# Small products on two halves of the PE array taken in turn, and two groups of transfers moved, in a two-layer hybrid block

## Chip, cores and metric

One core of a Trainium2 chip. The metric is the device time of one execution in microseconds; of several runs the median is given.

## What is computed

Two layers of a block with three token mixers in parallel, 256 tokens by 1024 features, in float32. The reference, cut to what matters here:

```python
for l in range(DEPTH):
    p = x @ w_in[l]
    y_a = rwkv7_time_mix(p[..., :o_mla], ...)      # linear attention with a state per head
    y_b = mla_branch(p[..., o_mla:o_s5], ...)      # causal softmax attention on latents
    y_c = s5_branch(p[..., o_s5:o_gate], ...)      # complex diagonal scan
    gates = jax.nn.sigmoid(p[..., o_gate:].reshape(bsz, t, N_BRANCHES, D_MODEL) + gate_b[l])
    merged = gates[..., 0, :] * y_a + gates[..., 1, :] * y_b + gates[..., 2, :] * y_c
    x = layer_norm(DEEPNORM_ALPHA * x + merged @ w_out[l], ln1_g[l], ln1_b[l])
    h = jax.nn.silu(x @ ffn_w1[l]) * (x @ ffn_w3[l])
    x = layer_norm(DEEPNORM_ALPHA * x + h @ ffn_w2[l], ln2_g[l], ln2_b[l])
```

In `rwkv7_time_mix` the decay and the step size come from two low-rank products (`tanh(dw) @ w2`, `da @ a2`), and the recurrence runs over the tokens; the kernel does it in chunks, with scores between the tokens of a chunk. In `s5_branch` the inputs of the scan are `einsum('btgc,gpc->btgp', ug, bb)`, real and imaginary, with 16 channels to a group.

## The kernel before

**Weights.** All weights come as 276 chunks of 128 x 1024 float32 (512 KB; eight of 416 KB), in the order in which they are used. `w_load` (L155 on) issues a chunk's transfer on SP's queue into `raw` (L160, three buffers), ACT casts it into `whi` (L161, four buffers), and DVE subtracts the two into `wlo` (L171; a part on POOL, L173). `w_next` keeps four chunks ahead. Each product with a weight is three PE products in turn, high by high, low by high, high by low (L206 to L208 in `mm3`; L510 to L512 in `token_major`). SP's queue is in order: what stands before a weight transfer holds it up.

**Order.** The program text gives each engine its order after a scheduler of the tile framework has placed the instructions; two tables of short names, ORDER1 (first half of a layer: the input projection and the scan) and ORDER2 (the linear attention, the attention, the outputs), say in which order generators are advanced, one pair for each layer. In ORDER1 `m` is the latents, `S0 S1` the projection of u, `P` and `T0` to `T4` the scan's tables, `N` the norm of the latents, `r0` to `r6` projections of the linear attention, `t0` to `t3` the first part of `s5_tile`, `w0` to `w3` its second part, `g` and `G` gates. `issue_after` keeps the instructions in its block behind a given one.

**Scan.** `s5_in` projects u and copies it on ACT, and when both halves are there shuffles u into `U2` by eight small transfers on SP's queue (L695), so that two groups of channels lie on rows 0 to 63 and two on rows 64 to 127. `s5_tables` makes the scan's tables: for layer 0 in the head of the kernel, with a chain of rotations on POOL (L385 to L389) and spreads of the B and C matrices on ACT (`bd`, `cd`, L418); for layer 1 during ffn1 of layer 0. Their temporary memory is used afterwards by others, `lg`, `lb` and `xk` among them. `s5_tile(F)` makes eight products of 64 rows (L726), four on the upper row half into one PSUM bank of tag `pa`, then four on the lower half into a second one; each bank is multiplied on DVE by the rotation tables (L733 to L736) as soon as its four are there. The tag `pa` has two banks, and all stages share them. A float32 product leaves two records in the trace.

**Linear attention.** For each f of four (two heads of 64 rows each): `prep(f)` makes the two low-rank products, w2 on rows 0 to 63 (L867) and a2 on rows 64 to 127 (L871), each into its own bank, each followed by a Tanh on ACT (L869, L873). `scores(f)` makes four products on the upper half (head 0) into one bank, a copy on ACT into `Mk` (the copies have the line of the helper, L113), masks on POOL (L947), and then the same for the lower half (L940).

**Output and norm.** `token_major` is the product with w_out (8 chunks) and with ffn_w2 (22 chunks) and the layer norm behind it. It loads the norm's gain and offset over 128 partitions (`lg`, L516, `lb`, L517, 512 KB each) and the residual (`xk`, L518, 1 MB: for the first layer's w_out from the input, else from `xd`, the copy that the norm before wrote to DRAM, L537). The text issues them before chunk 2 of w_out and before chunk 12 of ffn_w2; what they depend on is free earlier, and the scheduler places them where it finds room. The core of that (L516 to L518):

```python
            if k == at:
                SY.dma_start(out=lg, in_=lnv[l, ln:ln + 1, :].to_broadcast([128, D]))
                SY.dma_start(out=lb, in_=lnv[l, ln + 1:ln + 2, :].to_broadcast([128, D]))
                SY.dma_start(out=xk, in_=x_dram)
            w = w_next()
```

## Time and profile before

| | us |
|---|---|
| median of 3 runs | 1076.62 |
| the runs | 1078.77, 1067.44, 1076.62 |
| the profiled execution | 1068.97 |
| its span in the trace | 1067.1 |
| PE busy | 1014.2 |
| DVE busy | 784.7 |
| ACT busy | 482.6 |
| POOL busy | 235.2 |

The profile is of one execution: the span runs from the first to the last instruction in the trace, and the time of the execution has 1.9 us around it. "Busy" is the time in which an engine ran at least one instruction; the rest of the span it waited or had nothing to do. PE's matmuls overlap one another, so the time from one start to the next is shorter than the duration of one.

### The profile page before, as it was taken

The page shows a single profiled execution, that of the slowest core. Times are in us where ns is not written, and L with a number is a line of the kernel's source. Part 1 is how long each engine was busy: PE and PEld are TensorE (multiplying, and loading weights), DVE is VectorE, ACT ScalarE, POOL GpSimd, SP SyncE. Part 2 cuts the span into 40 slices and gives each one's busy share as a digit, 9 for nine tenths or more (in the row PEclk, how much of TensorE's full clock was granted, in tenths as well). Part 3 has the DMA queues.
Part 4 walks back from the last instruction along what each step waited for, and adds up shares of the span by engine and source line. Part 5 has one row for each costly group of instructions (what it writes and reads, how often), then busy time and mean ns, then how long its engine had stood idle before and what let it go on. Part 6 is the DMA issues. An engine that isn't in the chain of part 4 may idle for free.

```text
span 1067.1 us, 21219 instructions
## 1 busy us (share of the span) xinstructions
PE 1014.2 (95%) x8560; PEld 912.5 (86%) x8560; DVE 784.7 (74%) x1542; ACT 482.6 (45%) x797; POOL 235.2 (22%) x262
## 2 busy tenths in 40 slices
PE   8799989999999999799999999999999999999997
PEld 7798778888896999798878999778889879999885
DVE  7969978976578778386474998888747876667546
ACT  5544477534244244144325346865334423443431
POOL 2970222300000599500012003221002420000000
PEclk9989999999999999999999999999999999999999
DMA  8442241223385555466536325232234755555562
GB/s 280 156 159 90 91 147 41 92 89 100 93 294 177 197 180 171 162 207 217 185 123 218 126 81 191 79 98 85 76 100 173 252 190 215 183 188 183 179 196 79
DMA packets 47394, 163.86 MB, mean 154 GB/s; under 512 B 5696, under 2 KB 8256, under 8 KB 46400
## 3 DMA queue, kind: packets, MB, share of 16 engines
q1 hardware_dynamic: 47008, 161.98, 45.9%
q8 instruction: 67, 1.10, 0.4%
q10 hardware_dynamic: 288, 0.52, 0.1%
q14 instruction: 31, 0.25, 0.1%
HBM read 156.72 MB, written 4.19 MB: 151 GB/s over the span
## 4 chain that ended last, share of the span: by engine, by line
PE 58%; DVE 17%; POOL 9%; DMA 7%; ACT 5%; issue 3%; SPq 0%; DVEq 0%; ACTq 0%; POOLq 0%
PE mm L208 11%; PE mm L207 10%; PE mm L206 10%; DMA raw<-in_ws 6%; DVE wlo L171 3%; PE mm L511 3%; PE mm L512 3%; PE mm L510 3%; ACT whi L161 3%; DVE z L745 1%; PE pa L726 1%; PE pb L1035 1%; POOL st L387 1%; PE pb L1043 1%; PE pa L940 1%
## 5 line engine op out<-in xcount | busy, mean ns | idle before, releaser
L171 DVE TENSOR_TENSOR wlo<-raw,whi 128x1024 fp32r<-128x1024 f32 (+2 forms) x265 | 333.5, 1262 | 171.8 <-ACT whi L161 169.1
L161 ACT CAST whi<-raw 128x1024 fp32r<-128x1024 f32 (+2 forms) x267 | 277.4, 1043 | 379.8 <-PE mm L207 211.8
L206 PE MATMUL mm<-xh,whi 128*128 128x256 f32 x1312 | 376.9, 287 | 14.2 <-ACT whi L161 13.9
L208 PE MATMUL mm<-xh,wlo 128*128 128x256 f32 x1312 | 376.1, 287 | 2.9 <-DVE wlo L171 2.6
L207 PE MATMUL mm<-xl,whi 128*128 128x256 f32 x1312 | 375.1, 286 | 0.4 <-DVE xl L262 0.4
L206 PEld LDWEIGHTS mm<-xh,whi 128*128 128x128 f32 x1312 | 249.2, 190 | 18.6 <-ACT whi L161 14.5
L208 PEld LDWEIGHTS mm<-xh,wlo 128*128 128x128 f32 x1312 | 250.2, 191 | 7.6 <-DVE wlo L171 4.0
L207 PEld LDWEIGHTS mm<-xl,whi 128*128 128x128 f32 x1312 | 250.2, 191 | 2.7 <-DVE xl L262 0.6
L240 POOL TENSOR_TENSOR rs<-rs,mhalf 128x1 f32<-128x1 f32 x8 | 7.8, 971 | 341.2 <-DVE rs L238 341.2
L206 PE MATMUL mm<-yh,whi 128*128 128x256 f32 x256 | 74.6, 291 | 0.1
L207 PE MATMUL mm<-yl,whi 128*128 128x256 f32 x256 | 74.1, 289 | 0.0
L208 PE MATMUL mm<-yh,wlo 128*128 128x256 f32 x256 | 74.1, 289 | 0.0
L511 PE MATMUL mm<-wlo,hh 128*128 128x512 f32 x132 | 52.0, 394 | 0.0
L510 PE MATMUL mm<-whi,hh 128*128 128x512 f32 x132 | 51.7, 394 | 0.0
L512 PE MATMUL mm<-whi,hl 128*128 128x512 f32 x132 | 51.5, 392 | 0.0
L206 PEld LDWEIGHTS mm<-yh,whi 128*128 128x128 f32 x256 | 48.5, 189 | 2.3 <-ACT qa L113 0.9
L207 PEld LDWEIGHTS mm<-yl,whi 128*128 128x128 f32 x256 | 48.5, 190 | 1.2 <-issue 0.8
L208 PEld LDWEIGHTS mm<-yh,wlo 128*128 128x128 f32 x256 | 48.6, 190 | 1.1 <-issue 0.7
L240 POOL TENSOR_TENSOR rsn<-rsn,mhalf 128x8 f32<-128x8 f32 x4 | 6.5, 1634 | 142.8 <-DVE rsn L238 142.8
L173 POOL TENSOR_TENSOR wlo<-raw,whi 128x384 fp32r<-128x384 f32 (+2 forms) x24 | 27.7, 1162 | 44.6 <-ACT whi L161 42.5
L947 POOL TENSOR_SCALAR_AFFINE_SELECT Mk<-Mk 64x512 f32<-64x512 f32 x32 | 27.0, 844 | 43.6 <-ACT Mk L113 42.3
L510 PEld LDWEIGHTS mm<-whi,hh 128*128 128x128 f32 x132 | 24.8, 188 | 6.2 <-DVE th L1284 0.8
(487 smaller groups left out, 1745.7 us busy)
## 6 DMA issues: line engine op xcount, KB each, us to landing
raw<-in_ws SPq DMA_DIRECT2D x267, 512.0 KB, 3.8
raw<-in_ws SPq DMA_DIRECT2D x8, 416.0 KB, 3.5
xd<-xk SPq DMA_DIRECT2D x3, 1024.0 KB, 4.1
xk<-xd SPq DMA_DIRECT2D x3, 1024.0 KB, 7.4
lg<-in_lnv SPq DMA_DIRECT2D x4, 512.0 KB, 5.0
lb<-in_lnv SPq DMA_DIRECT2D x4, 512.0 KB, 5.7
pc<-in_spC SPq DMA_DIRECT2D x2, 768.0 KB, 5.3
pb<-in_spB SPq DMA_DIRECT2D x2, 512.0 KB, 4.9
```

What stands on the lines that cost most here:

```text
L161: S.copy(out=hi[:, s], in_=raw[:, s])
L171: V.tensor_tensor(out=lo[:, 0:m], in0=raw[:, 0:m], in1=hi[:, 0:m].bitcast(F32), op=ALU.subtract)
L173: G.tensor_tensor(out=lo[:, m:w], in0=raw[:, m:w], in1=hi[:, m:w].bitcast(F32), op=ALU.subtract)
L206: PE.matmul(ps, lhsT=wh, rhs=xh, start=first, stop=False)
L207: PE.matmul(ps, lhsT=wh, rhs=xl, start=False, stop=False)
L208: PE.matmul(ps, lhsT=wl, rhs=xh, start=False, stop=last)
L240: G.tensor_tensor(out=out, in0=in_, in1=mh(out), op=ALU.pow)
L387: E.tensor_tensor(out=s1, in0=c0, in1=ls, op=ALU.mult)
L510: PE.matmul(acc[b][n], lhsT=ah, rhs=w[0][:, s], start=(k == 0), stop=False)
L511: PE.matmul(acc[b][n], lhsT=ah, rhs=w[1][:, s], start=False, stop=False)
L512: PE.matmul(acc[b][n], lhsT=al, rhs=w[0][:, s], start=False, stop=(k == nk - 1))
L947: G.affine_select(out=Mk[r, h], in_=Mk[r, h], pattern=[[0, 4], [1, 2], [1, 64]], compare_op=ALU.is_ge, fill=0.0, base=-1, channel_multipli ...
```

## The change

Five edits.

1. A helper `in_turn` makes a list of products and chains each behind the one before with `issue_after`. `s5_tile`, `prep` and `scores` take both `pa` banks first and then make their products in turn, one on the upper row half, one on the lower. The DVE work, the Tanhs and the copies follow behind.
2. In ORDER1 of layer 1 `r0` stands before `N t0` instead of behind.
3. The eight shuffles of u are issued on ACT's queue instead of SP's.
4. `token_major` issues its loads behind a chunk's `w_next`, and after the last weight transfer that has been issued; `xk` is split in halves.
5. The loads are spread: in w_out over chunks 0 and 1 (first half of xk and lb; lg and second half), in ffn_w2 over chunks 9, 10, 11 and 12 (first half of xk, lg, lb, second half).

```diff
-    "m S0 S1 P N t0 r0 r1 r2 t1 r3 w0 w1 t2 t3 g0 r4 r5 w2 w3 G3 G1 G2 r6 G0 g1",
+    "m S0 S1 P r0 N t0 r1 r2 t1 r3 w0 w1 t2 t3 g0 r4 r5 w2 w3 G3 G1 G2 r6 G0 g1",
...
+            state["dma"] = SY.dma_start(out=raw[:, s], in_=ws[i, :, s])
...
+    def in_turn(mms):
+
+        last = None
+        for ps, lhsT, rhs in mms:
+            with tc.issue_after(inst(last)) if last is not None else ExitStack():
+                last = PE.matmul(ps, lhsT=lhsT, rhs=rhs, start=True, stop=True)
...
+        loads = [(xk[:, 0], x_dram[:, 0]), (lg, lnv[l, ln:ln + 1, :].to_broadcast([128, D])),
+                 (lb, lnv[l, ln + 1:ln + 2, :].to_broadcast([128, D])), (xk[:, 1], x_dram[:, 1])]
...
-            if k == at:
-                SY.dma_start(out=lg, in_=lnv[l, ln:ln + 1, :].to_broadcast([128, D]))
-                SY.dma_start(out=lb, in_=lnv[l, ln + 1:ln + 2, :].to_broadcast([128, D]))
-                SY.dma_start(out=xk, in_=x_dram)
             w = w_next()
+            if k in at:
+
+                with tc.issue_after(inst(state["dma"])):
+                    for o, i in loads[at.index(k)::len(at)]:
+                        SY.dma_start(out=o, in_=i)
...
-                        SY.dma_start(out=U2[r:r + 32, j // 2::2, :], in_=u[32 * j:32 * j + 32, :, i, :])
+                        S.dma_start(out=U2[r:r + 32, j // 2::2, :], in_=u[32 * j:32 * j + 32, :, i, :])
...
+                pss = [mxps("a"), mxps("a")]
+                in_turn([(pss[pp][:, 256 * qq + 128 * ri:256 * qq + 128 * ri + 128],
+                          bl[64 * pp:64 * pp + 64, 2 * F + qq, ri, :], U2[64 * pp:64 * pp + 64, 2 * F + qq, :])
+                         for qq in range(2) for ri in range(2) for pp in range(2)])
...
+                pss = [mxps("a"), mxps("a")]
+                in_turn([(pss[i][:, 0:256], w2a2[64 * i:64 * i + 64, 128 * f:128 * f + 128], ld[64 * i:64 * i + 64])
+                         for i in range(2)])
...
+                pss = [mxps("a"), mxps("a")]
+                in_turn([(pss[h][:, 128 * b:128 * b + 128],
+                          BK[64 * h:64 * h + 64, b // 2, 2 * (b % 2):2 * (b % 2) + 2].rearrange("p a t -> p (a t)"),
+                          AR[64 * h:64 * h + 64, :, b]) for b in range(4) for h in range(2)])
                 for h in range(2):
...
-            token_major(gate0[1], 8, 0, False, q, l, 2)
+            token_major(gate0[1], 8, 0, False, q, l, [0, 1])
...
-                token_major((hh, hl), NF, 2, l == layers - 1, q2, l, 12)
+                token_major((hh, hl), NF, 2, l == layers - 1, q2, l, [9, 10, 11, 12])
```

The lines of the changed kernel are shifted by 7 to 10: L160 and L161 stay, L206 to L208 become L213 to L215, L418 becomes L425, L518 becomes L529, L695 becomes L705, and all products in turn have the helper's line, L209.

SP's queue from the end of the first w_out to ffn_w2 of layer 0, before (`xd` is the copy of x behind a norm, `pb` an input of layer 1's tables, `raw` a weight chunk):

```order
L537 DMA xd_4219<-xk 128x2048
L160 DMA raw<-in_ws 128x1024 x3
L363 DMA pb<-in_spB 128x1024
L160 DMA raw<-in_ws 128x1024 x23
L516 DMA lg<-in_lnv 128x1024
L517 DMA lb<-in_lnv 128x1024
L518 DMA xk<-xd_4219 128x2048
L160 DMA raw<-in_ws 128x1024 x14
L160 DMA raw<-in_ws 128x832 x2
```
The same stretch of the queue now:

```order
L160 DMA raw<-in_ws 128x1024 x6
L547 DMA xd_4220<-xk 128x2048
L160 DMA raw<-in_ws 128x1024 x3
L370 DMA pb<-in_spB 128x1024
L160 DMA raw<-in_ws 128x1024 x37
L160 DMA raw<-in_ws 128x832 x2
L160 DMA raw<-in_ws 128x1024 x10
L529 DMA xk<-xd_4220 128x1024
L160 DMA raw<-in_ws 128x1024
L529 DMA lg<-in_lnv 128x1024
L160 DMA raw<-in_ws 128x1024
L529 DMA lb<-in_lnv 128x1024
```
Before, the three loads stood behind 23 weight transfers, in ffn1; now the first half of xk, lg, lb and the second half stand behind 49, 50, 51 and 52 transfers, in ffn_w2.

PE around the scores of f = 1 in layer 0, before (`kr__236,BK` are the scores, `ka,qa` products of the attention, `mm` products with weights):

```order
L207 MATMUL mm<-yl,whi 128x256
L926 MATMUL pa<-kr,c 128x256
L208 MATMUL mm<-yh,wlo 128x256
L940 MATMUL pa<-kr__236,BK 128x128 x4
L206 MATMUL mm<-yh,whi 128x256
L207 MATMUL mm<-yl,whi 128x256
L940 MATMUL pa<-kr__236,BK 128x128 x4
L1188 MATMUL pa<-ka,qa 128x128 x2
L208 MATMUL mm<-yh,wlo 128x256
L206 MATMUL mm<-yh,whi 128x256
```
The same scores now, in line L209:

```order
L215 MATMUL mm<-yh,wlo 128x256
L213 MATMUL mm<-yh,whi 128x256
L933 MATMUL pa<-kr,c 128x256
L214 MATMUL mm<-yl,whi 128x256
L209 MATMUL pa<-kr__236,BK 128x128
L215 MATMUL mm<-yh,wlo 128x256
L213 MATMUL mm<-yh,whi 128x256
L214 MATMUL mm<-yl,whi 128x256
L209 MATMUL pa<-kr__236,BK 128x128 x7
L215 MATMUL mm<-yh,wlo 128x256
L213 MATMUL mm<-yh,whi 128x256
```
Before there were two blocks of four, each on one row half, with two weight products between; now the first of the eight stands alone, and the other seven are one block behind three weight products.

ACT in the head of layer 0, before (`u` is the copy of the projection, `bd` and `cd` the spreads of the tables, `kr` a mix of the linear attention's inputs):

```order
L113 COPY u<-mm 128x2x128 x2
L161 CAST whi<-raw 128x1024
L418 ACTIVATE bd<-pb,c 128x32x16
L418 ACTIVATE cd<-pb,c 128x32x16 x2
L161 CAST whi<-raw 128x1024
L418 ACTIVATE bd<-pb,c 128x32x16
L593 ACTIVATE kr__236<-mm,dv 128x256
L418 ACTIVATE bd<-pb,c 128x32x16
L593 ACTIVATE kr__236<-mm,dv 128x256
L418 ACTIVATE cd<-pb,c 128x32x16 x2
L593 ACTIVATE kr__236<-mm,dv 128x256
L161 CAST whi<-raw 128x1024
```
The same part now, with the eight shuffles in it:

```order
L113 COPY u<-mm 128x2x128 x2
L705 DMA U_248<-u 32x4x128 x8
L161 CAST whi<-raw 128x1024 x2
L603 ACTIVATE kr__236<-mm,dv 128x256
L425 ACTIVATE bd<-pb,c 128x32x16
L425 ACTIVATE cd<-pb,c 128x32x16 x2
L603 ACTIVATE kr__236<-mm,dv 128x256
L161 CAST whi<-raw 128x1024
L603 ACTIVATE kr__236<-mm,dv 128x256
L161 CAST whi<-raw 128x1024
L425 ACTIVATE bd<-pb,c 128x32x16
L603 ACTIVATE kr__236<-mm,dv 128x256
```
Two weight casts now stand right behind the eight issues, before the second bd; before, one stood between the u copies and the second bd, the next behind the first pair of cd, and the next only behind the second pair.

## Rows read from the trace of the kernel before

**Rows 1.** The page: busy time, share of the span, instructions.
```profile
PE 1014.2 (95%) x8560; PEld 912.5 (86%) x8560; DVE 784.7 (74%) x1542; ACT 482.6 (45%) x797; POOL 235.2 (22%) x262
```

**Rows 2.** PE's timeline (start, us, line, operation, [idle before <-releaser]), three places.
```profile
51.35 0.58 PE L206 MATMUL mm<-xh,whi 128*128 128x256 f32 x1 [5.62 <-ACT whi L161]
...
453.54 0.58 PE L206 MATMUL mm<-xh,whi 128*128 128x256 f32 x1 [6.83 <-ACT whi L161]
...
581.61 0.68 PE L726 MATMUL pa<-U,bl 64*128 64x128 f32 x4 [2.26 <-DMA U<-u]
```

**Rows 3.** SP's DMA queue, timeline, ffn1 of layer 0.
```profile
426.88 0.33 SPq L160 DMA_DIRECT2D raw<-in_ws  x1
442.81 0.33 SPq L516 DMA_DIRECT2D lg<-in_lnv  x1
...
444.18 10.91 SPq L160 DMA_DIRECT2D raw<-in_ws  x4
```

**Rows 4.** POOL's timeline, the last instruction of the tables.
```profile
441.49 1.29 POOL L389 TENSOR_TENSOR st<-st,t 128x512 f32<-128x512 f32 x1
```

**Rows 5.** Stretch, busy time per engine, PEclk, DMA share, GB/s.
```profile
453.60:458.00 4.40, 3.93 (x17) 3.64 (x18) 4.30 (x7) 2.49 (x4) 0.00 (x0) 0.50 0.36 136
```

**Rows 6.** ACT's timeline, the head and layer 1 after the u copy.
```profile
48.67 1.33 ACT L418 ACTIVATE cd<-pb,c 128x512 f32<-128x512 f32 x2 [4.98 <-DVE pb L408]
...
50.27 1.03 ACT L161 CAST whi<-raw 128x1024 fp32r<-128x1024 f32 x1
...
579.49 1.09 ACT L161 CAST whi<-raw 128x1024 fp32r<-128x1024 f32 x1
```

**Rows 7.** Stretches as in Rows 5, the two scan stages.
```profile
100.00:125.00 25.00, 23.04 (x328) 19.85 (x330) 25.00 (x59) 10.28 (x19) 0.99 (x1) 1.00 0.13 43
...
600.00:650.00 50.00, 48.88 (x593) 44.21 (x592) 48.67 (x101) 20.01 (x31) 5.38 (x5) 1.00 0.32 105
```

**Rows 8.** SP's queue, the U shuffles of both layers.
```profile
33.37 6.92 SPq L695 DMA_DIRECT2D U<-u  x8
...
578.02 5.11 SPq L695 DMA_DIRECT2D U<-u  x8
```

**Rows 9.** POOL's timeline, the end of the rotation.
```profile
69.71 1.28 POOL L389 TENSOR_TENSOR st<-st,t 128x512 f32<-128x512 f32 x1
```

**Rows 10.** PE's timeline, blocks of small products (x counts records).
```profile
76.28 1.71 PE L726 MATMUL pa<-U,bl 64*128 64x128 f32 x16
...
157.96 2.01 PE L940 MATMUL pa<-kr__236,BK 64*128 64x128 f32 x16
...
174.33 1.16 PE L940 MATMUL pa<-kr__236,BK 64*128 64x128 f32 x8
...
583.60 0.71 PE L726 MATMUL pa<-U,bl 64*128 64x128 f32 x4
```

**Rows 11.** PE's timeline, low-rank products beside others.
```profile
122.19 0.48 PE L867 MATMUL pa<-ld,pc 64*128 64x256 f32 x1
122.20 0.48 PE L871 MATMUL pa<-ld,pc 64*128 64x256 f32 x1
...
192.44 0.82 PE L940 MATMUL pa<-kr__236,BK 64*128 64x128 f32 x5
193.00 0.48 PE L867 MATMUL pa<-ld,pc 64*128 64x256 f32 x1
```

**Rows 12.** DVE's timeline, first scan tile of layer 1.
```profile
586.25 0.69 DVE L733 TENSOR_TENSOR pa__6593<-pa,ct 128x512 f32<-128x512 f32 x1 [4.42 <-PE pa L726]
```

**Rows 13.** SP's queue, lg before the first wout.
```profile
292.60 0.33 SPq L160 DMA_DIRECT2D raw<-in_ws  x1
293.71 0.33 SPq L516 DMA_DIRECT2D lg<-in_lnv  x1
```

**Rows 14.** The page: DMA issues, KB each, us to landing.
```profile
xk<-xd SPq DMA_DIRECT2D x3, 1024.0 KB, 7.4
```

**Rows 15.** Instructions of tile Mk: copies out of PSUM, ns min/median/max.
```profile
L113 ACT COPY Mk<-pa x16: 561/586/589, 159.2 to 730.7; 128x512 f32<-128x512 f32 x16
```

More of the change, by code (lines that the diff above doesn't have):

```diff
@@ L159, in w_load @@
         for s in (slice(0, w // 2), slice(w // 2, w)) if i == 0 else (slice(0, w),):
-            SY.dma_start(out=raw[:, s], in_=ws[i, :, s])
+            state["dma"] = SY.dma_start(out=raw[:, s], in_=ws[i, :, s])
             S.copy(out=hi[:, s], in_=raw[:, s])
@@ L721, in s5_tile @@
                 sh4 = [128, 2, 2, 128]
+                pss = [mxps("a"), mxps("a")]
+                in_turn([(pss[pp][:, 256 * qq + 128 * ri:256 * qq + 128 * ri + 128],
+                          bl[64 * pp:64 * pp + 64, 2 * F + qq, ri, :], U2[64 * pp:64 * pp + 64, 2 * F + qq, :])
+                         for qq in range(2) for ri in range(2) for pp in range(2)])
                 for pp in range(2):
-                    ps = mxps("a")
-                    for qq in range(2):
-                        for ri in range(2):
-                            PE.matmul(ps[:, 256 * qq + 128 * ri:256 * qq + 128 * ri + 128],
-                                      lhsT=bl[64 * pp:64 * pp + 64, 2 * F + qq, ri, :],
-                                      rhs=U2[64 * pp:64 * pp + 64, 2 * F + qq, :], start=True, stop=True)
-                    ps4 = ps.rearrange("p (q r t) -> p q r t", q=2, r=2)
+                    ps4 = pss[pp].rearrange("p (q r t) -> p q r t", q=2, r=2)
                     a = q.tile(sh4, F32, tag="pa", name="pa_", bufs=3)
@@ L865, in prep @@
                     pr["bon"] = t1("bon", (128, 2, T), 2)
[L866 to L867 removed]
+                pss = [mxps("a"), mxps("a")]
+                in_turn([(pss[i][:, 0:256], w2a2[64 * i:64 * i + 64, 128 * f:128 * f + 128], ld[64 * i:64 * i + 64])
+                         for i in range(2)])
                 uu = t1("uu")
[L869 to L871 removed]
+                S.activation(out=uu, in_=pss[0][:, 0:256], func=AF.Tanh, bias=hw0[:, f:f + 1], scale=0.5)
                 ta = t1("ta")
[L873 removed]
+                S.activation(out=ta, in_=pss[1][:, 0:256], func=AF.Tanh, bias=ha0[:, f:f + 1], scale=0.5)
                 Gc = t1("Gc", (128, 4, 65))
@@ L935, in scores @@
                 Mk = t1("Mk", (128, 2, 4, 2, 64), NMK)
+                pss = [mxps("a"), mxps("a")]
+                in_turn([(pss[h][:, 128 * b:128 * b + 128],
+                          BK[64 * h:64 * h + 64, b // 2, 2 * (b % 2):2 * (b % 2) + 2].rearrange("p a t -> p (a t)"),
+                          AR[64 * h:64 * h + 64, :, b]) for b in range(4) for h in range(2)])
                 for h in range(2):
-                    o = slice(64 * h, 64 * h + 64)
-                    ps = mxps("a")
-                    for b in range(4):
-                        PE.matmul(ps[:, 128 * b:128 * b + 128],
-                                  lhsT=BK[o, b // 2, 2 * (b % 2):2 * (b % 2) + 2].rearrange("p a t -> p (a t)"),
-                                  rhs=AR[o, :, b], start=True, stop=True)
-                    cp(9, out=Mk[:, h].rearrange("p b a t -> p (b a t)"), in_=ps)
+                    cp(9, out=Mk[:, h].rearrange("p b a t -> p (b a t)"), in_=pss[h])
                     for i in range(2):
```

6 lines of the change are left out of this document (removed).

## Prediction

> **What bounds the kernel now.** I read the busy totals first: TensorE (PE) works 1014.2 of 1067.1 us [rows 1]. So there are only two ways down: fewer microseconds of PE work, or fewer of the some 50 us in which it stands or runs at half clock. Next I looked for the largest idle times in PE's timeline. The largest is 6.83 us, ended at 453.54 by the weight cast on ACT [rows 2]. Followed back through the queues: SP issues a weight transfer at 426.88, and its next instruction, the load of lg, only at 442.81 [rows 3]. In between SP held nothing but a wait, 15.60 us long (442.81 − 426.88 − 0.33). What ended it stands on POOL: the last instruction of the scan tables ends at 441.49 + 1.29 = 442.78 [rows 4], 0.03 us before; lg, lb and xk lie in memory that these tables used. The weight transfers behind lg in SP's queue start at 444.18, and PE ran out of weights. The stall costs more than its length: the granted clock is 0.50 (1.2 GHz) still from 453.6 to 458.0, where PE is again 3.93 of 4.40 us busy [rows 5].
>
> The second largest is 5.62 us at 51.35, in the head, also released by a weight cast [rows 2]. On ACT that cast stands at 50.27 behind two spreads (cd, 1.33 us) that waited 4.98 us for DVE [rows 6]. The third, 2.26 us at 581.61, waits for the shuffled U of layer 1 [rows 2].
>
> Third view, the busy time by stretch: in the two scan stages DVE is full, 25.00 of 25.00 and 48.67 of 50.00 us [rows 7]. PE work saved there is not time saved unless DVE starts sooner.
>
> **Part 1, the late residual loads in ffn2.** In layer 0 lg, lb and xk move from behind 23 weight transfers to behind 49 (one of the four halves after each of four chunks). At 442.78 the tables are done, long before; so the wait of 15.60 us goes, and with it 6.83 us of idle PE. The half clock: from 453.54 to 458.0 PE worked 4.46 us, at 0.50 that is some 2.2 us lost. I take their sum, −9 (bounds −9.5 with the short wait for the first wlo behind it, and −7, the idle time alone). Nothing new is late there: POOL's tables themselves are off the path.
>
> **Part 2, the U transfers from SP to ACT.** Eight issues took 6.92 us of SP's queue in the head and 5.11 us in layer 1 [rows 8], about 0.6 us each with one stall of 2.3 us. On SP the weight transfers stood behind them; on ACT the weight casts, mix-ins and spreads do. In the head the order changes with it: two casts now come before the bd and cd spreads, and the cast that came at 50.27 no longer waits behind cd. What limits the gain is POOL: its rotation chain, which works without a break, ends at 69.71 + 1.28 = 70.99 [rows 9], and the scan can't start before. I take −3.5: the idle 5.62 us and some 1.5 us of half clock, less half for ACT's 5 us of issues, which now delay the casts. Bounds −6 (all of it, and no loss) and +3 (casts 5 us late, two chunks ready). In layer 1, ACT issues eight times right after the u copy; the cast at 579.49 [rows 6] then comes at about 583, some 3.5 us later, where PE takes a new chunk each 3.9 us on the average (276 chunks in 1067 us). Against that r0 is now ahead of N and t0, so PE has some 17 more weight products (a chunk has 24: by the average at most 2.7 us) between u and the scan inputs and hardly meets the 2.26 us. I take 0 (bounds −3 and +4).
>
> A note on the page: the Trainium skill, "DMA: Bandwidth & Descriptors", section "Issuing engines are not separate DMA queues", says that issuing from several engines saves only the sequencer's time to initiate, usually small beside the transfer itself. [Rows 8] show that time to be not small here, 0.6 us an issue, and in a queue with others behind it. By the rule alone this part would be worth nothing, and the sum 3.5 us higher.
>
> **Part 3, the scores in turn.** A block is priced by its rows [rows 10]: 4 records (two products) last 0.71 us, 8 records (four products) 1.16, 16 records, one half and then the other, 2.01 for scores and 1.71 for scan inputs. So one product adds some 0.22 and the first costs some 0.27 more. That the halves run together is seen at 122.19 and 122.20: a product on rows 0 to 63 and one on rows 64 to 127 start 0.01 us apart, and at 193.00 a low-rank product starts inside a score block [rows 11]. Two products in turn then cost as one. Before, by the order of the instructions: two f in one block of eight, five and a half in blocks of four and one pair of twos, 2 × 2.01 + 11 × 1.16 + 2 × 0.71 = 18.2 us. After: seven times 1 + 7 and once 1 + 3 + 4, so eight singles at 0.49, seven at 1.16 (four of the seven lie on one half), a three and a four at 0.71: 3.9 + 8.1 + 1.4 = 13.4. Gain 4.8. The low-rank pairs lose: three products that ran free inside score blocks now stand alone, and five pairs are still cut 1 + 1; at some 0.7 us a block (0.71, that of two records longer) nine singles before against ten and a pair after, +1.4. Net −3.4. I take −3, a little less, since there are only two banks of this kind and both are now taken together. Bounds −5 (pairs free again) and +1 (below).
>
> **Part 4, the scan inputs in turn.** Of eight tiles four stood in one block of eight, two in 4 + 4, one in 5 + 3 and layer 1's first in four blocks of two: 4 × 1.71 + 4 × 1.16 + (1.16 + 0.94) + 4 × 0.71 = 16.4 us. After: four blocks of eight in turn, two of 1 + 7, one of 4 + 1 + 3 and one of 6 + 2: 4 × 1.16 + 2 × 1.65 + 1.91 + 1.43 = 11.3. On PE that is −5.1. But DVE is full there [rows 7], and it is DVE that uses the products. Only layer 1's first tile is different: DVE waited 4.42 us for it [rows 12]. Now it is 4, 1 and 3 with weight products between, so the second bank isn't sooner. I take −1 (bounds −5, all of PE's gain, and 0).
>
> **Part 5, the loads in the two wouts.** Here the loads move into the weight stream's tightest stretch. lg had waited 0.78 us at its old place (293.71 − 292.60 − 0.33) [rows 13], so nothing is gained by moving it. xk takes 7.4 us to land in the median [rows 14]; half of it twice beside weights delays one or two chunks. I take +1 (bounds 0 and +3: a landing doubled once per wout).
>
> Sum: −9 − 3.5 + 0 − 3 − 1 + 1 = −15.5 us against the profiled execution's 1068.97, so 1053.5. The median of the runs shown is 1076.62, 7.65 above it; carried over, 1061.1.
>
> **Rivals.** (a) Only the stall goes. The two banks are the limit: each score block's copy to Mk takes 0.586 us on ACT, sixteen of them [rows 15], and both banks must be free before the next eight. If each second copy is now bare, 8 × 0.59 = 4.7 us eat part 3 whole, and ACT's issues eat part 2. What speaks for it: parts 3 and 4 save work in the stretches where PE shares the bound. Against: weight products stand between and cover a part of a copy. Result −9 + 1 = −8: 1068.6, within 1%. Here the page "TensorEngine Tiling (Array Packing)", section "PSUM Bottleneck", of the Trainium skill speaks against the change: tiling speeds up the array and not the evacuation, so the copy may become the limit. The trace leaves that close: two copies are 1.17 us, the block that feeds them 1.16.
>
> (b) Part 2 turns against the kernel: ACT's eight issues hold up the casts in both layers. +3 in the head, +4 in layer 1, the rest as above: −9 + 3 + 4 − 3 − 1 + 1 = −5, 1071.6, within 1%. For it: casts stand right behind the issues. Against: in the head the raw data came long before it was cast.
>
> (c) Slower: the load at its new place blocks SP again, now in three places. If in a wout a half of xk finds its memory still held, as lg did, the weights behind it stop for as long as lg's, and each stall costs the 9.5 us of part 1. At one place the kernel merely stands at −6; it decides from two places on. With both wouts and one ffn2: −15.5 + 28.5 = +13, 1089.6. Against: the waits at the old place of the first wout were 0.78 us, and every load now comes 10 or more transfers later.
>
> (d) The change doesn't do what it says: the scheduler cuts the turns. The order already shows 1 + 7, which is in the sum; if the seven didn't overlap, part 3 is lost (+3) and part 4 with it (+1): 1065.1, faster by 1.07%, so barely; its chance of 0.05 is counted in (a).
>
> **How the numbers follow.** A difference of about 1% (10.8 us) is what a measurement of this kernel can tell. Chances: forecast as summed 0.65, (a) 0.18, (b) 0.10, (c) 0.07. The forecast's own spread: from the values taken to the lower bounds of the six terms it is 0.5, 2.5, 3, 2, 4 and 1 us, to the upper ones 2, 6.5, 4, 4, 1 and 2; taken as independent (root of the sum of squares) 6 below and 9 above, so 1055 to 1070. That the 7.65 us between profile and median carry over is a choice, as the runs of before lie 11.3 us apart; without it 1053.5, less 6 is 1047.5. The range reaches a little below that, and above over (a) and (b): 1046 to 1075. Faster by over 1% means below 1065.9, 4.8 above the forecast: some 0.87 of the forecast's 0.65, and the 0.03 or so of (a) that is (d), 0.60. Slower means above 1087.4: (c) and what (b) has at its end, 0.08. Within 1%: the rest, 0.32.
>
> **What would show it.** Right: SP without a wait over 3 us in ffn1 of layer 0, PE without the 6.83 us and the clock at 1.00 there; score blocks of 14 records that last 1.2 us; PE's sum of busy time lower by some 8 us. Wrong: an idle time of PE over 3 us that a weight cast ends within 10 us of the U issues; PE waiting for banks (ended by Mk copies) before the seven; SP blocked before xk in a wout; or a later end of POOL's rotation than 71.

## The result and the profile after

The changed kernel takes 1089.57 us in the median of four runs (1086.67 to 1093.72), the kernel before in the same series 1073.49: ratio 1.0151, 95% interval 1.0105 to 1.0196. The forecast was 1061.1, with a range of 1046 to 1075. A ratio is estimated over the executions that are not counted as slow, so it can differ from the quotient of the medians (e11 below: 1.0090 and 1.0145; e12: 1.0019 and 0.9984). The profiled execution has a span of 1085.0 us, 17.9 more than before. The totals of the page, to be put beside [rows 1]:

```profile
PE 1020.4 (94%) x8560; PEld 912.8 (84%) x8560; DVE 787.8 (73%) x1542; ACT 482.8 (44%) x797; POOL 236.6 (22%) x262
```

PE is busy 6.2 us longer, though it has the same 8560 records. The clock explains it: at half clock a product takes longer. So I split the time from the start of the first to the start of the last matmul of each trace into three: the idle times of PE; the time lost to the clock (active time times one minus the granted clock); and the rest, PE's work at full clock. All three are worked out from the trace's records. The third comes out too low where the clock fell for long: at half clock the products with a weight follow one another at 0.21 us, at full clock at 0.12 (the rows are in the last section), which is less than double. In e2 and e8, where no product was changed, it is 2.5 and 2.6 us below the kernel before.

| us of PE | before | after |
|---|---|---|
| idle | 44.0 | 55.9 |
| lost at half clock | 8.6 | 20.1 |
| work at full clock | 1005.2 | 999.9 |

By this measure the work fell by 5.3 us; with the half clock counted by the two paces above it is an estimated 4, where the forecast had some 8. Idle time and clock rose by 23.5. Where they did is shown by how late the same instruction comes in the two traces:

| landmark on PE | before | after | later by |
|---|---|---|---|
| last products of layer 0's scan | 125.4 | 126.5 | 1.1 |
| first scores of layer 0 | 158.0 | 160.9 | 2.9 |
| last scores of layer 0 | 209.5 | 221.9 | 12.4 |
| first product of the first wout | 319.3 | 330.6 | 11.3 |
| first product of ffn1 | 346.3 | 361.5 | 15.2 |
| ffn1 behind the second token half of the norm (L206, then L213) | 359.0 | 376.2 | 17.2 |
| first product of ffn2 | 487.7 | 495.4 | 7.7 |
| first scores of layer 1 | 678.8 | 690.1 | 11.3 |
| last scores of layer 1 | 730.3 | 750.6 | 20.3 |
| first product of the second wout | 842.7 | 856.6 | 13.9 |
| last product of ffn2, layer 1 | 1058.9 | 1077.0 | 18.1 |

From the first scores to the wout the two layers lose 8.4 and 2.6 us, the wouts with their norms 5.9 and 4.2, the stretches up to the first scores (head and scan) 2.9 and, from ffn2 on, 3.6. One place wins, 9.5 us: ffn1 of layer 0. The 20.3 at the last scores of layer 1 overstates the loss: 6.4 of it is back at the wout, since weight products had been done earlier, ahead of the scores.

In ffn1 SP's wait of 15.60 us is gone: in its queue's timeline, to be put beside [rows 3], fifteen weight transfers follow one another. The view merges them into one row; the longest time between two of their issues is 5.6 us, where it was 15.9. PE is full at full clock where it had stood: the stretch of 30 us (its length, then the busy time of PE, weight loads, DVE, ACT and POOL, then PEclk), beside [rows 5]:

```profile
425.14 44.17 SPq L160 DMA_DIRECT2D raw<-in_ws  x15
```

```profile
445.00:475.00 30.00, 30.00 (x253) 30.00 (x252) 24.06 (x29) 12.02 (x15) 15.40 (x10) 1.00 0.54 175
```

The scores themselves come out as priced: the time covered by their records is 18.15 us before and 13.39 now, the 4.8 that were worked out. In PE's timeline a block of seven products in turn (14 records) lasts as long as one of four on one half (beside [rows 10]):

```profile
183.96 0.49 PE L209 MATMUL pa<-kr__236,BK 64*128 64x128 f32 x2
...
184.93 1.16 PE L209 MATMUL pa<-kr__236,BK 64*128 64x128 f32 x14
```

But from the first scores to the last it now takes 61.0 and 60.5 us instead of 51.5 in both layers. The view lists the instructions of one line with first and last start; before, then after:

```profile
L940 PE MATMUL pa<-kr__236,BK x64: 272/272/373, 158.0 to 209.5; 64*128 64x128 f32 x64
...
L940 PE MATMUL pa<-kr__6305,BK x64: 272/272/373, 678.8 to 730.3; 64*128 64x128 f32 x64
```

```profile
L209 PE MATMUL pa<-kr__236,BK x64: 272/272/374, 160.9 to 221.9; 64*128 64x128 f32 x64
...
L209 PE MATMUL pa<-kr__6307,BK x64: 272/272/373, 690.1 to 750.6; 64*128 64x128 f32 x64
```

And there are new falls of the clock. In the stretches below the clock is 0.50 in the second half of layer 0's linear attention and behind the norms of both wouts; before, it was 1.00 in all three. Each costs at most 2.4 to 3.0 us, half of PE's busy time.

```profile
242.70:249.20 6.50, 5.99 (x59) 5.35 (x58) 3.24 (x18) 0.37 (x1) 0.00 (x0) 0.50 0.02 5
358.80:365.20 6.40, 4.86 (x15) 3.80 (x16) 5.70 (x12) 1.17 (x2) 1.00 (x1) 0.50 0.00 0
884.60:891.00 6.40, 5.69 (x17) 4.44 (x18) 5.70 (x14) 1.17 (x2) 1.00 (x1) 0.50 0.00 0
```

In PE's timeline the norm at the end of the first wout stands bare: 3.02 us of idle time, ended by DVE's last step on xk:

```profile
359.66 1.11 PE L497 MATMUL pa<-c,xk 128*128 128x128 f32 x4 [3.02 <-DVE xk L490]
```

And ACT's timeline, where U is issued now, shows the weight casts held back twice, 6.12 and 5.09 us (beside [rows 6] and [rows 8]); in PE's, the wait for U in layer 1 is still there, 2.71 us (beside [rows 2]). ACT in the head, ACT in layer 1, PE in layer 1:

```profile
33.29 6.33 ACTq L705 DMA_DIRECT2D U<-u  x8
39.66 1.99 ACT L161 CAST whi<-raw 128x1024 fp32r<-128x1024 f32 x2 [6.12 <-DMA U<-u]
```

```profile
585.77 5.21 ACTq L705 DMA_DIRECT2D U<-u  x8
591.11 1.04 ACT L161 CAST whi<-raw 128x1024 fp32r<-128x1024 f32 x1 [5.09 <-issue]
```

```profile
592.04 0.68 PE L209 MATMUL pa<-U,bl 64*128 64x128 f32 x6 [2.71 <-DMA U<-u]
```

### The profile page after: what moved, and what is told of

It is laid out like the page before. It is cut to its first block, busy times and chain, and to the rows that moved or that the text cites. A ratio compares the mean times of both kernels' runs of the same rounds, so it can differ in the third digit from the quotient of the medians.

```text
span 1085.0 us, 21227 instructions
## 1 busy us (share of the span) xinstructions
PE 1020.4 (94%) x8560; PEld 912.8 (84%) x8560; DVE 787.8 (73%) x1542; ACT 482.8 (44%) x797; POOL 236.6 (22%) x262
## 4 chain that ended last, share of the span: by engine, by line
PE 47%; DVE 10%; DMA 4%; ACT 2%; issue 2%; POOL 2%; ACTq 0%; DVEq 0%; POOLq 0%; SPq 0%
PE mm L213 10%; PE mm L215 9%; PE mm L214 9%; DMA raw<-in_ws 3%; PE mm L518 3%; PE mm L519 3%; PE mm L517 3%; DVE wlo L171 1%; PE mm L1299 1%; ACT whi L161 1%; DVE z L753 1%; PE mm L1300 1%; PE mm L1301 1%; PE pc L519 1%; PE pc L517 1%
## 5 line engine op out<-in xcount | busy, mean ns | idle before, releaser
L161 ACT CAST whi<-raw 128x1024 fp32r<-128x1024 f32 (+2 forms) x267 | 277.9, 1042 | 372.2 <-PE mm L214 217.5
L215 PE MATMUL mm<-xh,wlo 128*128 128x256 f32 x1312 | 375.4, 286 | 8.3 <-DVE wlo L171 8.2
L213 PE MATMUL mm<-xh,whi 128*128 128x256 f32 x1312 | 377.1, 287 | 2.7 <-ACT whi L161 2.3
L215 PEld LDWEIGHTS mm<-xh,wlo 128*128 128x128 f32 x1312 | 251.3, 192 | 13.7 <-DVE wlo L171 9.4
L213 PEld LDWEIGHTS mm<-xh,whi 128*128 128x128 f32 x1312 | 249.3, 190 | 8.1 <-ACT whi L161 3.0
L213 PE MATMUL mm<-yh,whi 128*128 128x256 f32 x256 | 74.4, 291 | 1.9 <-ACT yh L113 0.9
L215 PE MATMUL mm<-yh,wlo 128*128 128x256 f32 x256 | 73.6, 288 | 0.0
L213 PEld LDWEIGHTS mm<-yh,whi 128*128 128x128 f32 x256 | 48.5, 190 | 5.0 <-ACT yh L113 1.4
L518 PE MATMUL mm<-wlo,hh 128*128 128x512 f32 x132 | 52.0, 394 | 0.0
L519 PE MATMUL mm<-whi,hl 128*128 128x512 f32 x132 | 51.5, 393 | 0.0
L215 PEld LDWEIGHTS mm<-yh,wlo 128*128 128x128 f32 x256 | 48.6, 190 | 1.6 <-issue 0.7
L518 PEld LDWEIGHTS mm<-wlo,hh 128*128 128x128 f32 x132 | 24.8, 188 | 6.0 <-DVE wlo L171 0.6
```

The costliest lines, as they stand in the source:

```text
L161: S.copy(out=hi[:, s], in_=raw[:, s])
L213: PE.matmul(ps, lhsT=wh, rhs=xh, start=first, stop=False)
L215: PE.matmul(ps, lhsT=wl, rhs=xh, start=False, stop=last)
L518: PE.matmul(acc[b][n], lhsT=ah, rhs=w[1][:, s], start=False, stop=False)
L519: PE.matmul(acc[b][n], lhsT=al, rhs=w[0][:, s], start=False, stop=(k == nk - 1))
```

## The experiments

Each kernel is the kernel before with a part of the change, unless said otherwise. How the change moves the order was read from the built programs, and decided which parts to take apart: the ffn2 loads move SP's queue alone; the scores alone move 669 rows of PE, nearly all that the whole change moves.

| run | part | us | ratio (95%) |
|---|---|---|---|
| e1 | ffn2 loads late | 1066.35 | 0.9917 (0.9884 to 0.9951) |
| e2 | wout loads late | 1081.36 | 1.0048 (1.0006 to 1.0090) |
| e3 | scores in turn | 1087.70 | 1.0133 (1.0078 to 1.0188) |
| e4 | U on ACT, r0 first | 1080.28 | 1.0038 (1.0005 to 1.0071) |
| e5 | ffn2, scan inputs, pairs | 1065.27 | 0.9938 (0.9908 to 0.9968) |
| e6 | e5 and r0 first | 1061.05 | 0.9895 (0.9859 to 0.9931) |
| e7 | scores chained, not in turn | 1087.91 | 1.0161 (1.0102 to 1.0220) |
| e8 | wout loads over four chunks | 1082.95 | 1.0124 (1.0065 to 1.0183) |
| e9 | e2, order of the products held | 1083.54 | 1.0103 (1.0017 to 1.0188) |
| e10 | scores in turn, f = 3 | 1075.81 | 1.0016 (0.9977 to 1.0056) |
| e11 | scores in turn, f = 0 | 1089.31 | 1.0090 (1.0031 to 1.0149) |
| e12 | all but the scores | 1072.03 | 1.0019 (0.9977 to 1.0060) |

**e1, the ffn2 loads.**

```diff
-                token_major((hh, hl), NF, 2, l == layers - 1, q2, l, 12)
+                token_major((hh, hl), NF, 2, l == layers - 1, q2, l, [9, 10, 11, 12])
```

> The kernel before with one part of the change: the loads of lg, lb and xk in ffn2 moved to chunks 9 to 12, in both layers. Only SP's order differs from before. Theory A (each part acts in its own place): SP's wait of 15.60 us in ffn1 of layer 0 goes, PE's idle 6.83 us and the half clock behind it go, the span is 9 to 10 us shorter, ratio about 0.991. Rival B (the weights run out anyway, a chunk or two later): under 3 us shorter, ratio 0.997 or more, with a new idle time of PE in ffn1 or ffn2.

Measured: ratio 0.9917, 8.9 us of the 1076.03 of this series. In SP's timeline the longest time between two issues is 5.6 us, and in the table of stretches PE is full at clock 1.00 where it had stood:

```profile
426.62 27.49 SPq L160 DMA_DIRECT2D raw<-in_ws  x10
```

```profile
430.00:460.00 30.00, 30.00 (x252) 30.00 (x251) 24.12 (x29) 12.02 (x15) 15.20 (x10) 1.00 0.54 175
```

Theory A holds. Nothing is late a chunk later: from the first product of ffn1 to the first of ffn2 the trace of e1 has 131.9 us for 141.4 before, 7.3 of idle time and 2.0 of clock less.

**e2, e8, e9: the loads in the wouts.** e2 is the change's own part:

```diff
-            token_major(gate0[1], 8, 0, False, q, l, 2)
+            token_major(gate0[1], 8, 0, False, q, l, [0, 1])
```

> The kernel before with one part of the change: the loads of lg, lb and xk in both wouts moved to chunks 0 and 1. Theory A: the 2 MB of loads, issued within 3 us, double the landing times of the three weight transfers beside them (8 to 10 us for 4.3), the last chunks of wout come late, the layer norm of the first half starts only behind all products, PE is idle some 3 us at its end and then at half clock for some 7 us: +5.5 us at each of the two wouts, span +11, ratio about 1.010. Rival B (the end of wout is late for what comes before it, the linear attention's new order): span within 3 us, ratio 0.997 to 1.003.

Measured: +5.2 us (1.0048), with an interval of 0.6 to 9.7: above rival B's forecast and half of theory A's +11. In PE's timeline the norm is bare as in the changed kernel, though the linear attention is in the old order; so rival B's cause falls:

```profile
345.50 0.66 PE L497 MATMUL pa<-c,xk 128*128 128x128 f32 x4 [3.02 <-DVE xk L490]
```

In the trace of e2 the three weight transfers issued beside the loads land after 8.3, 9.7 and 7.2 us, in the kernel before all of this stretch after 4.1 to 4.6. Was it the burst? e8 spreads the loads (`[0, 1, 2, 3]`):

> The kernel before with the loads in both wouts late, but one of the four halves behind each of chunks 0 to 3 instead of two behind each of 0 and 1. Theory A (four loads within 3 us double the landing of the weights beside them): landings of weights stay under 7 us and the idle time of 3 us at the norm shrinks to 1 or 2, ratio 1.000 to 1.003. Rival B (any load there delays the norm, by the bytes alone): idle 3 us at the norm as with two chunks, ratio 1.004 to 1.008.

Measured: 1.0124, no better, and above what either theory gave; the landings are 5.8 to 6.3 us as hoped, and in PE's timeline the idle time at the norm is longer:

```profile
351.00 1.33 PE L497 MATMUL pa<-c,xk 128*128 128x128 f32 x5 [5.19 <-DVE xk L490]
```

So the burst is not it. The order of the built program offered another cause: with the loads late, the scheduler takes the last four chunks one by one over all four PSUM banks, where before it took them bank by bank and closed the first token half early. e9 chains the old order (`tail` holds the products issued so far):

```diff
+                with tc.issue_after(inst(tail[-1])) if tail and nk == 8 else ExitStack():
                     for i in range(NST):
                         run(wst[i], nk - NST + i, b, (n,))
```

> The loads of both wouts late behind chunks 0 and 1, as in the run with that part alone, but the products of the last four chunks are chained in the order of the kernel before: bank by bank, so that the first token half closes early. The spread loads had shown that landings are not it (under 7 us there, and the idle time at the norm 5.19 us). Theory A2 (the scheduler, which sees the weights come late, takes the last products chunk by chunk, all four banks close together, and the norm stands bare): no idle time at the norm over 1 us, ratio 0.998 to 1.003. Rival B2 (the weights really come late): PE waits for a weight cast in wout 3 us or more in sum instead, ratio 1.004 to 1.008.

Measured: 1.0103. The idle time at the norm is gone from PE's timeline, and PE waits for weight casts instead, 1.06 and 2.77 us:

```profile
321.98 0.73 PE L519 MATMUL mm<-whi,msh 128*128 128x512 f32 x2 [1.06 <-ACT whi L161]
...
335.87 0.80 PE L519 MATMUL mm<-whi,msh 128*128 128x512 f32 x1 [2.77 <-ACT whi L161]
```

Theory A2 falls and B2 holds, though the ratio is a little above its range (the interval takes it in): the weights really come late when 2 MB of loads share the stream in the 25 us of a wout, however they are spread and in whichever order PE takes the products. In the kernel before, these loads had run some 25 us earlier, beside products of the outputs. In the traces of e2 and e9 the first wout loses 5.3 and 5.8 us, the second 4.2 and 2.5, by landmarks ahead of and behind them. That is 8 to 10 us in a trace (10.1 in that of the changed kernel), the upper end of what the times of e2 allow.

**e3, e7, e10, e11: the scores.** e3 is the change's own part:

```diff
-                for h in range(2):
-                    o = slice(64 * h, 64 * h + 64)
-                    ps = mxps("a")
-                    for b in range(4):
-                        PE.matmul(ps[:, 128 * b:128 * b + 128],
...
+                pss = [mxps("a"), mxps("a")]
+                in_turn([(pss[h][:, 128 * b:128 * b + 128],
...
+                          AR[64 * h:64 * h + 64, :, b]) for b in range(4) for h in range(2)])
```

> The kernel before with one part of the change: the scores' products in turn over both banks, chained. By the order this alone moves 669 rows of PE's and 351 of DVE's, nearly all that the whole change moves. Theory A: PE's work is 2 to 5 us less, but weight products stand earlier and the chain of the linear attention is left bare, with more short idle times of PE between 125 and 300 us and two or three more falls of the clock there: span +8 to +14, ratio 1.008 to 1.013. Rival B (the in-turn products are a gain and the loss comes from low-rank pairs, scan inputs or U): span -3 to -5, ratio 0.996.

Measured: 1.0133, +14.3 us: theory A. The scores' records cover 13.39 us as in the changed kernel; PE's work at full clock is 1000.5 us by the measure above, 4.7 less (an estimated 3 with the paces); idle 52.4, lost to the clock 22.9. The second half of the linear attention shows what the time went to: in PE's timeline four waits for DVE and ACT, and in the table of stretches the clock at 0.56:

```profile
234.00 0.37 PE L1066 MATMUL pb<-ST,BKt 128*64 128x64 f32 x1 [0.70 <-DVE ST L113]
...
235.90 0.66 PE L1042 MATMUL pb<-S,kr__236 128*64 128x128 f32 x2 [0.78 <-DVE S L1070]
...
238.92 1.11 PE L1054 MATMUL pb<-Gc,DTf 64*64 64x64 f32 x8 [0.51 <-ACT Gc L113]
...
245.01 0.65 PE L1230 MATMUL pc<-PT,vt 128*64 128x256 f32 x2 [0.57 <-ACT PT L113]
```

```profile
232.50:242.50 10.00, 8.01 (x76) 6.56 (x76) 6.77 (x31) 0.37 (x1) 0.00 (x0) 0.56 0.17 55
```

Before, more weight products stood there. In the program, 706 weight products stand ahead of the first scores of layer 0 in both kernels; ahead of the last scores it is 891 before and 955 in e3, and between these and the last output of the linear attention 296 before and 201 in e3 (in layer 1, which loses less, 324 and 328). As I read it, the first product in turn takes one bank of two and holds it until the second is free and all eight are done; while attention and low-rank products wait for banks, the scheduler fills with weight products, and these are missing later, where the solve is a chain of short steps. That banks are why the scheduler fills is not shown; in the traces of e3 and of the changed kernel no idle time of PE's matmuls over 0.15 us is ended by a copy to `Mk`. It is the alternation that moves the order: in e10 below three of the four scores take both banks too, but keep the halves one after the other, and the weight products ahead of f = 1, 2 and 3 are those of before, 747, 822 and 889. e7 tests the order alone: all eight chained, so placed nearly as in e3, but few of them together. Its diff and those of e10 and e11 are against e3.

```diff
-    in_turn([... for b in range(4) for h in range(2)])
+    in_turn([... for b, h in [(0, 1), (0, 0), (1, 0), (2, 0), (3, 0), (1, 1), (2, 1), (3, 1)]])
```

> The kernel before with the scores' eight products chained, one of the second half first, then four of the first half and three of the second: both banks are held from the start as in the change, but the halves hardly run together. The order of the weight products is moved as in the change (935 of them before the layer's last scores, for 891 before and 955 in the change; in layer 1 3308 for 3261 and 3321). Theory A (the loss is the weight products that come too early): as slow as the scores in turn or slower, ratio 1.010 to 1.018, PE's work at full clock as before, 1005 us. Rival B (what costs is that products on two halves slow one another): ratio 0.998 to 1.003.

Measured: 1.0161; work at full clock 1003.9, and the scores' records cover 16.2 us. So the loss comes with the order. The products in turn save PE work, but that they take back a part of the loss isn't shown: the intervals of e3 and e7 overlap. e10 and e11 put one of the four scores in turn (e11 with `f == 0`); the others are chained, one half behind the other:

```diff
-    in_turn([... for b in range(4) for h in range(2)])
+    in_turn([... for b, h in ([(b, h) for b in range(4) for h in range(2)] if f == 3 else [(b, h) for h in range(2) for b in range(4)])])
```

> Scores in turn for f = 3 alone, the other three as before. The order is moved little: 897 weight products ahead of the last scores of layer 0 for 891 before, 3267 for 3261 in layer 1. Theory A (loss by weight products that come too early): no loss, ratio 0.997 to 1.002. Rival B (each set of scores in turn costs by itself, a quarter of 14 us): ratio 1.003 to 1.004.

> Scores in turn for f = 0 alone. The order is moved by more than half of what all four move it: 927 weight products ahead of the last scores of layer 0 for 891 before (955 with all four), 3296 for 3261 (3321). Theory A: more than half of the loss, 7 to 9 us, ratio 1.006 to 1.010. Rival B: a quarter, ratio 1.003 to 1.004.

Measured: 1.0016 and 1.0090, as theory A has it; e10's interval also takes in rival B's 1.003 to 1.004, e11's holds it at its edge. And e11's ten executions lie apart: three at 1075.6 to 1077.5 us with a mean granted clock of 0.983 to 0.987, seven at 1087.2 to 1101.8 with 0.958 to 0.978; the profiled one is of the seven. So e11's time alone doesn't part the order from the clock. The traces are sharper than the times. The scores' line in e11, layer 0 and layer 1, first and last start in us:

```profile
L209 PE MATMUL pa<-kr__236,BK x64: 271/272/374, 154.1 to 213.3; 64*128 64x128 f32 x64
...
L209 PE MATMUL pa<-kr__6305,BK x64: 272/272/374, 689.0 to 744.7; 64*128 64x128 f32 x64
```

| run | weight products before the last scores, layer 0, 1 | first to last scores, us | ratio |
|---|---|---|---|
| before | 891, 3261 | 51.5, 51.5 | 1 |
| e10 | 897, 3267 | 52.5, 52.5 | 1.0016 |
| e11 | 927, 3296 | 59.2, 55.7 | 1.0090 |
| e7 | 935, 3308 | 63.1, 58.0 | 1.0161 |
| e3 | 955, 3321 | 61.0, 60.5 | 1.0133 |

The stretch goes with the weight products that come too early, not with the number of scores in turn (1 in e10 and e11, 4 in e3, none in e7). By itself it is no loss, as it holds work that is then not done later. The loss is what is left at the first product of the wout. From the first scores to there, in us against before, worked out from the records:

| run | layer 0: longer by | idle | clock | layer 1: longer by | idle | clock |
|---|---|---|---|---|---|---|
| e10 | 2.8 | 4.0 | 0 | −0.9 | −0.5 | 0 |
| e11 | 6.9 | 5.8 | 1.7 | 10.0 | 1.2 | 10.2 |
| e7 | 9.5 | 6.1 | 3.3 | 3.2 | 2.8 | 0 |
| e3 | 8.9 | 6.6 | 4.4 | 2.6 | 2.7 | 0 |
| the change | 8.4 | 7.0 | 3.2 | 2.6 | 2.8 | 0 |

What is not idle or clock is PE's work. In layer 0 the idle time grows with the weight products that are missing between the last scores and the last output (32 in e10, 67 in e11, 70 in e7, 95 in e3). In layer 1 it doesn't (26, 19 and 31 missing, 4 more in e3), and e11 loses 10 us there to one fall of the clock that no other of these traces has.

**e4, U on ACT**, with `r0` ahead of `N t0` in layer 1:

```diff
-                        SY.dma_start(out=U2[r:r + 32, j // 2::2, :], in_=u[32 * j:32 * j + 32, :, i, :])
+                        S.dma_start(out=U2[r:r + 32, j // 2::2, :], in_=u[32 * j:32 * j + 32, :, i, :])
```

> The kernel before with one part of the change: the U shuffles issued on ACT, and r0 ahead of N and t0 in layer 1. Theory A: the head loses one idle time (5.62 us at 51) and gets two others (3.0 and 4.4 us), layer 1 keeps a wait for U of 2 to 3 us and gets a fall of the clock behind it: span 0 to +3, ratio 1.000 to 1.003. Rival B (casts behind the eight issues are what makes the changed kernel slow): span +6 or more, ratio 1.006 or more.

Measured: 1.0038, +4.1, a little above what A gave; the interval reaches into rival B's. In ACT's timeline of the head the cast behind the issues has waited 6.78 us, and in PE's the wait for U in layer 1 is 4.54 us, longer than before:

```profile
32.42 6.98 ACTq L708 DMA_DIRECT2D U<-u  x8
39.44 1.99 ACT L161 CAST whi<-raw 128x1024 fp32r<-128x1024 f32 x2 [6.78 <-DMA U<-u]
```

```profile
588.25 1.61 PE L739 MATMUL pa<-U,bl 64*128 64x128 f32 x8 [4.54 <-DMA U<-u]
```

That wait is not ended by a cast but by U itself. In the trace of e4 a weight transfer, no longer held behind the shuffles in SP's queue, is issued between them at 581.71 and lands at 587.90, and from the second shuffle on they land only at 588.12 to 589.26. The view of the tile in layer 1, before and then e4 (no run tests this alone):

```profile
DMA to landing us min/median/max: 2.0/2.1/3.3
```

```profile
DMA to landing us min/median/max: 3.2/5.1/6.7
```

**e5 and e6, what is left.** e5 takes the ffn2 loads and the in-turn products of scan inputs and pairs; e6 adds `r0`, with U still on SP:

```diff
-    "m S0 S1 P N t0 r0 r1 r2 t1 r3 w0 w1 t2 t3 g0 r4 r5 w2 w3 G3 G1 G2 r6 G0 g1",
+    "m S0 S1 P r0 N t0 r1 r2 t1 r3 w0 w1 t2 t3 g0 r4 r5 w2 w3 G3 G1 G2 r6 G0 g1",
```

> The kernel before with three parts of the change: the late loads in ffn2, the scan inputs in turn, the low-rank pairs in turn; scores, U and wout as before. Theory A: the -8.9 us of the ffn2 loads alone (ratio 0.9917) stay, the scan inputs give at most 1 to 2 us as DVE sets the pace there, the pairs nothing: ratio 0.988 to 0.992. Rival B (every in-turn product costs by its order, the scan's too): the gain is halved or more, ratio 0.996 or above.

> As the run before it, and r0 ahead of N and t0 in layer 1 as in the change, but U still issued on SP. If the wait for U in layer 1 (2.3 to 3.2 us of idle PE and in three of five profiles some 14 us at half clock behind it) is met by the projection r0 in between, the idle time at the scan inputs goes under 1 us, no half clock follows, ratio 0.982 to 0.988. Rival: U comes late for the scan whichever products stand ahead, ratio as of the run before it, 0.988 to 0.992.

Measured: e5 0.9938, between its two theories, and its interval overlaps that of e1. PE's work is 3.1 us below e1's (1001.4 for 1004.5): the scan inputs' records cover 13.2 us for 16.4, the pairs' 9.8 in both. None of it shows in the time: DVE is busy for 25.00 of the 25 us from 100 to 125 in both traces. e6: 0.9895, 11.3 us, the fastest of all, though its interval overlaps that of e5. The ratio is the one that its rival gave, but the mechanism is the first: in PE's timelines the wait for U is 0.55 us where e5 has 3.40, and no half clock follows; e5, then e6:

```profile
575.32 0.46 PE L209 MATMUL pa<-U,bl 64*128 64x128 f32 x2 [3.40 <-DMA U<-u]
```

```profile
575.31 1.05 PE L209 MATMUL pa<-U,bl 64*128 64x128 f32 x8 [0.55 <-DMA U<-u]
```

**e12, from the other side**: the whole change without the scores in turn. Against the changed kernel:

```diff
-                in_turn([(pss[h][:, 128 * b:128 * b + 128],
...
+                for h in range(2):
...
+                    for b in range(4):
+                        PE.matmul(ps[:, 128 * b:128 * b + 128],
```

> The whole change without the scores in turn. If the parts add as they were measured alone, -8.9 for ffn2, +5.2 for wout, +4.1 for U and some +2 for scan inputs and pairs: ratio 1.000 to 1.005, against 1.0151 with the scores. Rival (the scores lose only beside the others, or the others only beside the scores): 1.008 or more, or 0.995 or less.

Measured: 1.0019, as forecast, and both rivals lie outside its interval. Taken from the whole, the scores are worth 0.0132, 14 us, as they were alone. And the parts add up: −8.9 (e1), +5.2 (e2), +14.3 (e3), +4.1 (e4) and +2.2 (e5 against e1, within its error) make +16.9 us; the whole change has +16.2 (0.0151 of 1073.49). The intervals of the parts leave such a sum open by some 9 us either way.

## Why the prediction was wrong

- **Part 1, the ffn2 loads**: forecast −9, measured −8.9, and 9.5 between the two ends of ffn1 in the trace of e1. Right in mechanism and size: the chain from PE's idle time over ACT's cast and SP's wait to POOL's last table instruction was the cause, and half clock behind the stall belonged in the sum. The sign "SP without a wait over 3 us" was too strict: up to 5.3 us are left between two issues, and PE doesn't meet them.
- **Part 2, U to ACT**: forecast −3.5 in the head and 0 in layer 1, measured +4.1. The steps that failed are "less half for ACT's 5 us of issues, which now delay the casts" and, for layer 1, "hardly meets the 2.26 us". In the trace of e4 ACT's queue holds the casts for 6.78 and 5.13 us, and in the head the one idle time of 5.62 us became three, 1.40, 2.95 and 4.37. Only the first of them ends with a cast; the other two end with `wlo` on DVE, which had stood 5.72 us without a cast and then did its table steps ahead of these `wlo`. By the end of layer 0's scan e4 is 1.4 us later than before. In layer 1 PE waits not for a cast but for U (4.54 us), which lands late beside a weight transfer, and from 587.0 on the clock is at 0.50 for 13.7 us. So rival (b) had the sign, and in the head the cause, but not the cause in layer 1. The 0.6 us an issue were read correctly from [rows 8]. The half of the edit that was good, r0 first, shows with U on SP (e6 against e5, 4.6 us); U on ACT without it was not run. The Trainium skill's sentence on issuing engines ("DMA: Bandwidth & Descriptors", section "Issuing engines are not separate DMA queues") promised hardly a gain and was right on that; that there was a loss it doesn't say.
- **Part 3, scores in turn**: forecast −3 with pairs, bounds −5 and +1; measured +14.3 for the scores. This is the main error. The step "Net −3.4. I take −3, a little less, since there are only two banks" priced the blocks, and the scores' came out as priced: 18.15 us became 13.39 (4.8 less was worked out). The loss of 1.4 us at the pairs did not come (9.8 before, 9.2 in the changed kernel). What had no term in the sum was what the scheduler does with the rest: I read only the block sizes from the order. That the same scores of f = 1 stand behind 794 weight products instead of 747, and the last ones behind 955 instead of 891, stood in it too. Rival (a), copies to Mk as the limit (the Trainium skill's "TensorEngine Tiling (Array Packing)", section "PSUM Bottleneck"), isn't borne out: in the changed kernel no idle time of PE's matmuls over 0.15 us is ended by such a copy. By my reading its resource, the PSUM banks, is the right one, but at work in the scheduler and not on the chip.
- **Part 4, scan inputs**: forecast −1 in time and −5.1 in PE's work; e5 against e1 shows −3.1 of work for scan inputs and pairs together (−5.1 + 1.4 = −3.7 worked out) and no gain in time. That agrees with the forecast and its reason, DVE; but the interval would hide 1 us, and the scan inputs were not run without the pairs.
- **Part 5, wout loads**: forecast +1, bounds 0 and +3; measured +5.2 (e2), and 8 to 10 by the landmarks of the traces. Mis-sized: I took one landing doubled per wout. In the trace three weight transfers in a row land late, and behind the idle time the clock falls, as it did in part 1, where I had counted it.
- **Rival (c)** gave 1089.6, the measured time almost exactly, and is wrong: SP never blocks before a half of xk (the gaps there are 0.05 us). A number that fits is not a mechanism.

What stays open: in the trace of e3 the two stretches from the first scores to the wout lose 11.5 us: 9.3 of idle time and 4.4 of the clock, less 2.2 of PE's work. The rest up to 14.3 lies within the interval of the times (8 to 20 us) and can't be placed: the profiled execution of e3 also has the long fall of the clock behind the wait for U (last section), and so have those of e2, e4, e8 and e9, where the scores are as before. Whether the falls follow from the idle times each time is not shown either; no run here holds the clock.

## What to carry to other kernels

When an edit passes through a scheduler, price the order and not the edit: count what stands ahead of the last link of the longest chain, before and after, and ask where the filling work is then missing. Alternating over two buffers to run two products together frees neither before the last product, and here, where others use these buffers, it moved the order, at a cost of 14 us (the scores). Moving a transfer was a gain where it took a wait out of a queue (ffn1), and a loss where it went into a stretch whose weights come just in time (wout), onto an engine whose queue works just in time (ACT), or out of a queue in which it had kept others from running beside it (U).

## What the runs showed of the hardware

The same kind of wait can cost nothing or some 7 us. Behind PE's wait for U in layer 1 (2.3 to 4.5 us) the granted clock stayed at 1.00 in the profiled execution of the kernel before, fell for some 3 us in that of the changed kernel, and for 17 us in e9, where PE was busy almost all along. The stretch behind the wait, before and in e9:

```profile
582.30:600.00 17.70, 17.70 (x141) 16.75 (x141) 12.99 (x25) 7.32 (x10) 0.00 (x0) 1.00 0.49 160
```

```profile
587.40:603.90 16.50, 16.45 (x67) 14.91 (x68) 7.78 (x13) 2.94 (x4) 0.00 (x0) 0.50 0.29 88
```

The pace of the products shows it too. In PE's timeline they start 0.12 us apart before, and 0.21 or 0.22 us apart in e9:

```profile
583.04 0.28 PE L207 MATMUL mm<-xl,whi 128*128 128x256 f32 x1
583.16 0.29 PE L208 MATMUL mm<-xh,wlo 128*128 128x256 f32 x1
```

```profile
589.58 0.42 PE L215 MATMUL mm<-xh,wlo 128*128 128x256 f32 x1
589.80 0.41 PE L213 MATMUL mm<-xh,whi 128*128 128x256 f32 x1
```

By these paces 16.45 us of busy PE at clock 0.50 are some 7 us lost. Falls of 13.7 to 17.1 us stand there in the traces of e2, e3, e4, e7, e8, e9, e10 and e11; in e1, e5, e6, e12, the changed kernel and the kernel before they are 0 to 6.8 us long. All five traces with the late ffn2 loads are among these; with one trace of each kernel that can be chance. Single executions of one kernel differ by more than most parts of this change are worth (the kernel before: 1064.96 to 1081.21 in the last series), and the parts could only be told apart by medians, and by landmarks within a trace. The Trainium skill, "TensorE: Matmul & The Clock Gate", says in "Part 1: The HAM clock gate" that the clock is low after idle time and that activity brings it back; the fall in e9 agrees, the 16.5 us at half clock of a busy PE do not.
